# A list scheduler with smaller charges per operation and 90 disturbed restarts

## The chip, the cores and the metric

The kernel runs on all 8 cores of one Trainium2 chip, each on its own 4096 tokens. The metric is the device time of the slowest core, in microseconds (us). The runs of one kernel lie close together: eleven of before took 1242.38 to 1245.46 us. Other runs were slower, most of them with a lower clock on one die: two runs of before, of 1479.74 and 1497.95 us, had 0.81 to 0.84 on cores 4 to 7. Such runs are marked slow and set aside. Cores 0 to 3 are one die and 4 to 7 the other. Each session ran on one chip, with the kernel before beside the others, and only runs of one session are compared.

## The reference

A token mixer (a gated convolution of width 3, and a spatial gating over blocks of 128 positions), an output projection, and a channel mixer with squared ReLU. The argument is about the channel mixer:

```python
h2 = rmsnorm(x, norm2_g[l])                                   # x: (4, 8192, 1024)
a = jax.nn.relu(jnp.einsum('bsd,df->bsf', h2, w_up[l]))       # 1024 -> 4096
x = x + jnp.einsum('bsf,fd->bsd', a * a, w_down[l])           # 4096 -> 1024, plus the residual
...
return rmsnorm(x, final_g)
```

## The kernel before

The program does not write its instruction streams by hand. It declares some thousands of operations with their reads and writes; a list scheduler places them on five queues (TensorE, ScalarE, VectorE, and the POOL and SP queues that issue DMAs). What each operation costs is an estimate in the program:

```python
def act(out, in_, func, reads, writes, n=MT, **kw):
    aps = sum(1 for v in kw.values() if not isinstance(v, (int, float)))
    S.add("act", ..., occ=(n / 1.2 + 200 + 70 * aps) / 1000, ...)     # us; the result is usable 0.09 later

def dve(fn, reads, writes, n=MT, rate=1, src=None):
    S.add("dve", fn, reads=reads, writes=writes, occ=(n / rate + 151) / 960, ...)
```

`occ` is how long the engine is taken and `dur` when the result is usable. A DMA is planned at 290 GB/s, all of them one after another, plus 2 us, plus a margin that the call chooses:

```python
def place(self, ops, phys, lat=0.12, dma_lat=2.0, dma_rate=290e3):    # forward pass
    ...
            if op.dma_key is not None:
                dma_free = max(dma_free, st + op.occ) + op.nbytes / dma_rate
                op.finish = dma_free + dma_lat + op.margin
            else:
                op.finish = st + op.dur - op.occ + occ
```

`place` takes, at each engine's next free moment, the ready operation with the smallest key. `push` runs backward through the order and sets each key to the latest start that still meets the end. The two alternate 9 times and the order with the lowest estimated finish is kept. Of all this only the order goes to the chip: the program writes each engine's list and the semaphores that it waits for.

Two matrix multiplications use a form with 7 products in place of 8, so each weight block of 4 parts must be extended by three VectorE sums to 7. At its first use a block of the down projection comes in as f32 on the POOL queue, is converted to f16 on the way (1 MB of f32 by the program, 512 KB at the destination in the DMA view), summed in place in one of six `RING` buffers and then stored for later:

```python
def combine(p, dst, src, dkeys, reads, margin):
    i, lkey, skey = dkeys
    dma("pool", p[:, 0:4, :, :], src[i % 16]..., reads, p.keys(0, 4), lkey, 4 * 128 * 2048, margin=margin)
    tt(p[:, 4, :, :], p[:, 3, :, :], p[:, 2, :, :], ALU.add, ...)            # "RING <- RING" in the traces
    tt(p[:, 3:6:2, :, :], ..., p[:, 3:5, :, :], ALU.subtract, ...)
    tt(p[:, 6, :, :], p[:, 1, :, :], p[:, 5, :, :], ALU.add, ...)
    dma("sp", dst, p[:, :, :, :], ...)

def load_w(n):
    s, i = wslot(), plan[n]
    if n < 32 and 16 <= i < 24:                       # first use of a down block: load and sum
        combine(RING[s], ws(i), wdn_d, (i, ("fl", s), ("fs", s)), [], 5.0)     # margin 5 us
    else:                                             # stored before: 7 parts, 896 KB, on the SP queue
        dma("sp", RING[s][:, :, :, :], ws(i), ..., margin=2.0)

def load_r(g, o_):                                    # residual: 8 loads a pair of token tiles, into RA and RB
    for h in range(2):
        dma("pool", R[h][:, o_::4, :], x1_d[m]..., ("rl", h, o_), 4 * 128 * 2 * MT, margin=4.0)

def up_unit(q, s):                                    # products into PSUM banks bA, bC, bD
    ...
    prod(bA, P1, True, False); snap(2, bA)            # ScalarE copies the bank to SN
    prod(bD, P2, True, True);  add(2, bD)             # VectorE adds the bank to SN: frees it
    ...
```

The matmuls write into PSUM (PS in the traces), which the program divides into banks; by its semaphores a matmul that is to start a new result waits until its bank has been read out. So VectorE holds two kinds of work in one list: additions that free PSUM banks for TensorE, and weight sums that wait for a DMA.

## Time and profile before

The kernel took 1246.82 us (median of 3, 1246.3 to 1248.05).

| | before |
|---|---|
| TensorE busy, slowest core | 97% of 1244.9 us |
| before the first matmul, all cores | 6.8 to 8.3 us |
| TensorE's stalls and half-clock matmuls before 80 us | 12 to 20 us |
| TensorE's excess from 80 us to the last weight matmul, slowest core | 0.02 us |
| after the last weight matmul | 16.5 to 17.6 us |

The excess is worked out from the trace: the sum, over consecutive matmuls, of the time between their starts less what a matmul needs at a granted clock of 1.00 (in the median 216 ns for 512 columns, 52 ns for 128 and 25 ns for 32, in before). The 5880 matmuls come to some 1200 us. Half-clock matmuls are those at a granted clock of 0.50: on core 7 from 31.70 to 38.53 us, where 512 columns take 427 ns.

From the page of before: busy time, share of the span and instructions of TensorE, then its busy share and its granted clock in tenths over 40 slices.

```profile
PE 1209.6 (97%) x5880; PEld 548.5 (44%) x5880; DVE 893.4 (72%) x1377; ACT 530.4 (43%) x905; POOL 86.0 (7%) x146
...
PE   5899999999999999999999999999999999999994
...
PEclk9899999999999999999999999999999999999998
```

The chain of work that ended last, in order of time (start, us, what), before:

```profile
68.66 1158.35 PE PS L424 x5536
...
1227.10 0.06 DVE RA L439
```

TensorE alone carries the chain from 68.7 to 1227 us.

The table by stage (window, us, busy time and instructions of each engine, granted clock, DMA share, GB/s), core 7:

```profile
core 7: us, PE busy (x) PEld busy (x) DVE busy (x) ACT busy (x) POOL busy (x), PEclk, DMA share, GB/s
...
484.00:491.00 7.00, 7.00 (x34) 3.17 (x33) 5.79 (x9) 3.76 (x7) 0.55 (x1) 1.00 0.99 202
491.00:498.00 7.00, 7.00 (x35) 3.17 (x33) 6.52 (x12) 5.07 (x10) 0.94 (x2) 1.00 0.64 117
```

### The profile page before, as it was taken

To read this page: it belongs to the slowest core of one execution; us is meant where nothing else is said; L and a number is where in the kernel's file an instruction comes from. 1 tells how busy PE (TensorE), PEld (TensorE's weight loads), DVE (VectorE), ACT (ScalarE), POOL (GpSimd) and SP (SyncE) were. 2 spreads that over 40 slices of the span, in tenths; PEclk is the share of its full clock that TensorE was granted. 3 is DMA by queue.
4 is the path that set the end of the run, shared out by engine and by line. 5 is a ranking of instruction groups with operands and counts; after the bars stand their busy time and mean duration, and the time that the engine had idled before them with its cause. 6 is when DMAs were issued, how large, how long until landed. Compare 5 with 4: busy or idle time off the path is not lost.

```text
span 1244.9 us, 18564 instructions; the slowest of 8 cores (1235.7 to 1244.9 us)
## 1 busy us (share of the span) xinstructions
PE 1209.6 (97%) x5880; PEld 548.5 (44%) x5880; DVE 893.4 (72%) x1377; ACT 530.4 (43%) x905; POOL 86.0 (7%) x146
## 2 busy tenths in 40 slices
PE   5899999999999999999999999999999999999994
PEld 3444444444444444444444444444444444444442
DVE  2778687877878887658759737767846876855746
ACT  4544655536554356026127205317405406503524
POOL 0100000000001011000101200000110000110000
PEclk9899999999999999999999999999999999999998
DMA  8968688596675869975577764576984645985423
GB/s 185 171 148 232 167 228 231 148 245 175 179 220 153 279 213 207 237 266 176 169 260 228 262 212 162 211 237 177 295 272 148 216 165 182 279 271 177 149 90 135
DMA packets 55183, 253.81 MB, mean 204 GB/s; under 512 B 6192, under 2 KB 6320, under 8 KB 54832
## 3 DMA queue, kind: packets, MB, share of 16 engines
q1 hardware_dynamic: 35152, 180.27, 42.8%
q0 software_dynamic: 19936, 72.36, 25.3%
q8 instruction: 49, 0.80, 0.3%
q14 instruction: 46, 0.38, 0.1%
HBM read 211.71 MB, written 65.01 MB: 222 GB/s over the span
## 4 chain that ended last, share of the span: by engine, by line
PE 93%; DMA 5%; DVE 1%; issue 0%; SPq 0%; DVEq 0%; POOLq 0%
PE PS L424 93%; DMA WSB_109<-bsf 2%; DMA X_74<-xT 1%; DMA X_73<-xT 1%; DMA WV<-wv 1%; DMA WCXB_53<-wcxb 1%; DVE RA L439 0%; DVE RB L439 0%; SPq L450 0%; DVE WU L446 0%; DVEq L344 0%; DVE FSQ_102 L439 0%; DVE FSQ_101 L439 0%; DVE Z L439 0%; DVEq L284 0%
## 5 line engine op out<-in xcount | busy, mean ns | idle before, releaser
L439 DVE TENSOR_TENSOR RB<-PS,RB 128x512 f32<-128x512 f32 x128 | 87.4, 690 | 91.4 <-PE PS L424 88.9
L424 PE MATMUL PS<-YN,WO 128*128 128x512 f16 x512 | 113.8, 379 | 0.0
L439 DVE TENSOR_TENSOR RA<-PS,RA 128x512 f32<-128x512 f32 x96 | 66.1, 690 | 60.6 <-PE PS L424 59.2
L439 DVE TENSOR_TENSOR A_89<-A_89 128x512 bf16<-128x512 bf16 (+1 forms) x192 | 94.5, 508 | 8.2 <-ACT A_89 L431 3.6
L431 ACT ACTIVATE SN_92<-PS 128x512 f32<-128x512 f32 x63 | 37.4, 595 | 106.5 <-PE PS L424 104.7
L424 PEld LDWEIGHTS PS<-YN,WO 128*128 128x128 f16 x512 | 50.1, 98 | 60.4
L424 PE MATMUL PS<-A_89,RING_83 128*128 128x512 bf16 x308 | 76.1, 379 | 0.0
L424 PE MATMUL PS<-A_89,RING_85 128*128 128x512 bf16 x308 | 76.1, 379 | 0.0
L424 PE MATMUL PS<-A_89,RING_86 128*128 128x512 bf16 x308 | 75.8, 379 | 0.0
L424 PE MATMUL PS<-A_89,RING_84 128*128 128x512 bf16 x308 | 75.5, 379 | 0.0
L424 PE MATMUL PS<-H_96,RING_87 128*128 128x512 f16 x308 | 75.1, 379 | 0.0
L424 PE MATMUL PS<-H_96,RING_83 128*128 128x512 f16 x308 | 74.5, 379 | 0.0
L424 PE MATMUL PS<-H_96,RING_88 128*128 128x512 f16 x308 | 74.3, 379 | 0.0
L424 PE MATMUL PS<-H_96,RING_84 128*128 128x512 f16 x308 | 74.3, 379 | 0.0
L431 ACT ACTIVATE SN_90<-PS 128x512 f32<-128x512 f32 x66 | 39.2, 595 | 76.7 <-PE PS L424 75.6
L424 PE MATMUL PS<-A_89,RING_88 128*128 128x512 bf16 x280 | 69.4, 379 | 0.0
L424 PE MATMUL PS<-A_89,RING_87 128*128 128x512 bf16 x280 | 69.1, 379 | 0.0
L431 ACT ACTIVATE SN_93<-PS 128x512 f32<-128x512 f32 x64 | 38.2, 596 | 71.8 <-PE PS L424 71.3
L424 PE MATMUL PS<-H_96,RING_85 128*128 128x512 f16 x280 | 67.9, 379 | 0.0
L424 PE MATMUL PS<-H_96,RING_86 128*128 128x512 f16 x280 | 67.4, 379 | 0.0
L431 ACT ACTIVATE SN_91<-PS 128x512 f32<-128x512 f32 x63 | 37.5, 595 | 70.1 <-PE PS L424 68.0
L439 DVE TENSOR_TENSOR SN_92<-PS,SN_92 128x512 f32<-128x512 f32 x63 | 43.4, 690 | 27.4 <-PE PS L424 22.7
(231 smaller groups left out, 2029.2 us busy)
## 6 DMA issues: line engine op xcount, KB each, us to landing
RING_83<-ws_s SPq DMA_DIRECT2D x21, 896.0 KB, 6.0
RING_84<-ws_s SPq DMA_DIRECT2D x21, 896.0 KB, 6.4
RING_87<-ws_s SPq DMA_DIRECT2D x20, 896.0 KB, 5.3
RING_88<-ws_s SPq DMA_DIRECT2D x20, 896.0 KB, 6.2
RING_85<-ws_s SPq DMA_DIRECT2D x19, 896.0 KB, 6.0
RING_86<-ws_s SPq DMA_DIRECT2D x19, 896.0 KB, 6.3
ws_s<-PREP_65 SPq DMA_DIRECT2D x12, 896.0 KB, 6.3
ws_s<-PREP_66 SPq DMA_DIRECT2D x12, 896.0 KB, 5.6
```

The costliest lines, as they stand in the source:

```text
L424: ins = e.matmul(real(o_), lhsT=l, rhs=r, start=st, stop=sp, skip_group_check=True)
L431: S.add("act", lambda e: e.activation(out=out, in_=real(in_), func=func, **kw), reads=reads, writes=writes, occ=(n / 1.2 + 200 + 70 * aps) ...
L439: dve(lambda e: e.tensor_tensor(out=out, in0=real(in0), in1=in1, op=op), reads, writes, n, rate, in0)
```

## The change

The intent is a truer model and a better search. The charge of a VectorE operation on 512 f32 elements goes from 691 to 601 ns, and of a ScalarE operation from 627 to 497 ns. The time until a result is usable is kept (780 and 717 ns). Then the best order's keys are disturbed 90 times with a spread of 0.3 us, and the lowest estimated finish wins. No instruction, byte or buffer is added or removed; only orders, PSUM banks and waits move.

```diff
-    def schedule(self, phys, rounds=8):
+    def schedule(self, phys, rounds=8, tries=90):
...
+        rnd = random.Random(1)
         best = None
-        for _ in range(rounds + 1):
...
+        for t in range(tries + 1):
+            if t:
+                for o, k in best[5].items():
+                    o.key = k if o.fixed else k + rnd.gauss(0, 0.3)
+            for _ in range(3 if t else rounds + 1):
...
+                order = self.place([op for op, _ in base], phys)
+                if len(order) < len(base):
+                    break
+                est = max(o.finish for o in order)
+                if best is None or est < best[0]:
+                    best = (est, order, ..., keys)
+                self.push(order, est)
...
-        assert len(order) == len(ops)
...
-                  occ=(n / 1.2 + 200 + 70 * aps) / 1000, banks=...)
+                  occ=(n / 1.2 + 70 + 70 * aps) / 1000, dur=(n / 1.2 + 290 + 70 * aps) / 1000,
+                  banks=...)
...
-            S.add("dve", fn, reads=reads, writes=writes, occ=(n / rate + 151) / 960,
-                  banks=...)
+            S.add("dve", fn, reads=reads, writes=writes, occ=(n / rate + 65) / 960,
+                  dur=(n / rate + 237) / 960, banks=...)
```

More of the change, by code (lines that the diff above doesn't have):

```diff
@@ L1 @@
 import contextlib
+import random
 import numpy as np
@@ L110, in add @@
         return op
-    def schedule(self, phys, rounds=8):
+    def schedule(self, phys, rounds=8, tries=90):
         base = [(op, op.deps) for op in self.ops]
+        rnd = random.Random(1)
         best = None
-        for _ in range(rounds + 1):
-            for op, deps in base:
-                op.deps = deps
-                for b in op.banks:
-                    b.left = len(b.ops)
-            order = self.place([op for op, _ in base], phys)
-            est = max(o.finish for o in order)
-            if best is None or est < best[0]:
-                best = (est, order, [(o, o.deps) for o in order],
-                        [(o.opens, o.opens.phys) for o in order if o.opens is not None],
-                        {o: (o.start, o.finish) for o in order})
-            self.push(order, est)
+        for t in range(tries + 1):
[3 more added lines that the diff above has]
+            for _ in range(3 if t else rounds + 1):
+                for op, deps in base:
+                    op.deps = deps
+                    for b in op.banks:
+                        b.left = len(b.ops)
+                keys = {op: op.key for op, _ in base}
+                order = self.place([op for op, _ in base], phys)
[3 more added lines that the diff above has]
+                if best is None or est < best[0]:
+                    best = (est, order, [(o, o.deps) for o in order],
+                            [(o.opens, o.opens.phys) for o in order if o.opens is not None],
+                            {o: (o.start, o.finish) for o in order}, keys)
+                self.push(order, est)
         self.est_total, self.ops = best[:2]
@@ L431, in act @@
             S.add("act", lambda e: e.activation(out=out, in_=real(in_), func=func, **kw), reads=reads, writes=writes,
-                  occ=(n / 1.2 + 200 + 70 * aps) / 1000, banks=[in_.bank] if isinstance(in_, Late) else [])
+                  occ=(n / 1.2 + 70 + 70 * aps) / 1000, dur=(n / 1.2 + 290 + 70 * aps) / 1000,
+                  banks=[in_.bank] if isinstance(in_, Late) else [])
         def dve(fn, reads, writes, n=MT, rate=1, src=None):
-            S.add("dve", fn, reads=reads, writes=writes, occ=(n / rate + 151) / 960,
-                  banks=[src.bank] if isinstance(src, Late) else [])
+            S.add("dve", fn, reads=reads, writes=writes, occ=(n / rate + 65) / 960,
+                  dur=(n / rate + 237) / 960, banks=[src.bank] if isinstance(src, Late) else [])
         def tt(out, in0, in1, op, reads, writes, n=MT, rate=1):
```

## The prediction

> **What bounds the kernel now.** TensorE, almost perfectly. The page's busy line gives it 97% of 1244.9 us, but matmul records overlap (379 ns each), so I read start-to-start times in the trace of the slowest core. From 80 us to the last weight matmul at 1227.5 us, a 512-column matmul follows its predecessor after about 216 ns; the total excess there is 0.02 us. At that pace the 5880 matmuls add up to 1200 us. The other 45 us are edges: 7.9 us before the first matmul, 20 us of stalls and half-clock matmuls before 80 us, 17.4 us of tail after the last weight matmul. On other cores the startup excess is 12 to 18 us, the tail 16.5 to 17.6. VectorE (72%) and ScalarE (43%) have slack: in the stage table VectorE is busy 301 of 378 us at its fullest.
>
> **What the change does.** It adds and removes no instruction, byte or buffer. It changes numbers of the program's own scheduler, hence the order on each engine, the PSUM banks and the waits. VectorE's charge for a 512-element f32 operation falls from 691 to 601 ns, ScalarE's from 627 to 497; the time until a result is usable stays (780 and 717 ns). Then the best order is disturbed 90 times and the lowest modelled finish kept.
>
> **Is the new charge truer?** Yes. VectorE's 512-element f32 operations reading PSUM have records of 691 ns but, when dense, 598 to 601 ns start-to-start; ScalarE's 597 and 478 ns (PSUM), 627 and 519 ns (SBUF). [...] One charge becomes too small: a 384-element weight scaling is charged 168 ns and takes 228.
>
> **How much lies on the critical path.** In the middle 1150 us, nothing: the chain of waits shows one run of matmuls from 68.7 to 1227 us, and no order changes their pace. Only edges can gain.
> - Startup: DMA engines are 93 to 100% busy from 8 to 72 us and weight loads are issued in a fixed chain, so the longest stalls (3.1 us for a convolution weight, 2.2 us for the u weight) end with a landing plus a scaling. Order can remove perhaps 1 to 3 us, such as a u scaling stuck behind a bias addition that waited for a late load. But the scheduler assumes 290 GB/s where startup moves 156 to 203, so its gains carry over poorly: -1.5 us.
> - Tail: final stores fill the DMA engines from 1230.6 to 1241.5 us. The first half stored starts being scaled at 1228.6, though its sums were ready by 1225; an earlier start is worth at most 2.5 us: -1 us.
> - Middle: less slack could open short stalls: +0.2 us.
>
> The optimum is a model's, and the slowest of eight cores decides.
>
> **Predicted time.** 1244.0 us against 1246.82; 8 in 10 within 1238.0 to 1249.0. Faster by over 2%: 2%; within 2%: 96%; slower by over 2%: 2%.
>
> **What would show it.** Right: instruction counts and mean durations unchanged; TensorE's excess between 80 us and the last weight matmul under 1 us; startup excess and tail each shorter by 0 to 3 us. Wrong: matmul gaps waiting for VectorE or ScalarE in the middle (model too optimistic), or startup excess moving by over 5 us (order matters there more than DMA).
>
> **What would make it wrong.** An order with waits for late loads ahead of needed VectorE work, holding TensorE or dropping its clock, or PSUM banks reused too tightly: 5 to 20 us lost. A gain over 2% would need 25 of the 45 edge microseconds.

The dropping clock can be seen in the trace of before: on core 7 the granted clock was 0.50 from 31.70 to 38.53 us, during and after a stall of TensorE of 2.90 us (by the view) that ended at 33.63.

## More of the kernel before

Below, a load lands when the last of its data is reported to be in place (its landing is given in us after its issue), and the slack behind it is the time from there to the first instruction that needs it.

What POOL issued before that, in the timeline of before (start, us, queue, line, operation, tiles, count, idle time before and what ended it):

```profile
463.50 2.84 POOL L450 DMA_DIRECT2D RB<-x_s  x4 [29.67 <-PE PS L424]
466.33 1.41 POOL L450 DMA_DIRECT2D RA<-x_s  x2
468.80 0.70 POOL L450 DMA_DIRECT2D RA<-x_s  x1 [1.06 <-DMA x_s<-X_74]
473.44 0.57 POOL L450 DMA_DIRECT2D RING_86<-wdn  x1 [3.93 <-PE PS L424]
474.01 0.70 POOL L450 DMA_DIRECT2D RA<-x_s  x1
```

SP's timeline in the same stretch, before:

```profile
452.67 0.32 SPq L450 DMA_DIRECT2D RING_84<-ws_s  x1
```

The DMA issues of 445 to 475 us, before (tiles, queue, operation, count, KB each at the destination, us from issue to landing):

```profile
RING_84<-ws_s SPq DMA_DIRECT2D x1, 896.0 KB, 5.7
RING_86<-wdn POOLq DMA_DIRECT2D x1, 512.0 KB, 14.8
```

VectorE's timeline when it comes to the first sum of this block, before:

```profile
492.98 0.69 DVE L439 TENSOR_TENSOR SN_90<-PS,SN_90 128x512 f32<-128x512 f32 x1
493.58 0.42 DVE L439 TENSOR_TENSOR RING_86<-RING_86 128x512 f16<-128x512 f16 x1
```

Seven residual loads go out ahead of the first down weights. The weights land at 473.44 + 14.8 = 488.2 us; VectorE comes to their first sum at 493.58, 5.3 us later, and no idle time stands beside it. That gap does not show as a cost or as a gain in any summary. It is slack.

The other cores of this profile have less of it. On core 0 the first down weights took 24.2 us and the second block's 24.4, and TensorE stalled there for 2.78 us, at a granted clock that stayed at 1.00, waiting for the second block itself:

```profile
494.98 1.89 PE L424 MATMUL PS<-A_89,RING_85 128*128 128x512 bf16 x8 [2.61 <-DMA RING_85<-wdn]
```

(The view counts the gap from the modelled end of the last matmul; the stalls in the text are start to start, less 216 ns, and so 0.16 to 0.17 us longer.)

## The result, and the profile after

The kernel after took 1251.88 us in the median of its three fast runs (1251.07, 1251.88 and 1253.61; with one slow run of 1338.3 the median is 1252.74, and a fifth run, 1283.38, was slow too). Before took 1247.13 beside it (1246.3 to 1248.05, 4 runs). The ratio is 1.004, with a 95% interval of 1.0021 to 1.006. Ratios are the mean time of one kernel's fast runs over that of the other's of the same rounds, so not quite the ratio of the medians. The kernel became about 5 us slower, and the predicted gain of 2.8 us and range up to 1249 did not hold.

The page of after, the slowest core (core 2, 1249.5 us). 67 matmul records are missing, so its busy time is not compared with before's.

```profile
PE 1205.5 (96%) x5813; PEld 548.4 (44%) x5880; DVE 896.7 (72%) x1377; ACT 527.3 (42%) x905; POOL 85.5 (7%) x146
...
PE   5899999999999998999999999999999999999994
...
PEclk9899999999999999999999999999999999999997
```

One slice of TensorE's row, the sixteenth (468 to 500 us), dropped from 9 to 8. In the waits of after (engine and tile that waited, for what: us in total, times, longest us), two lines are new:

```profile
DVE RING_86 L449 <- DMA RING_86<-wdn: 5.9, 1, 5.9
...
PE PS L433 <- DVE SN_90 L449: 5.7, 1, 5.7
```

The chain of after in that stretch, in order of time (lines of the program are 9 or 10 further down than before):

```profile
439.80 26.35 PE PS L433 x122
...
466.70 28.07 DMA RING_86<-wdn
...
494.94 0.06 DVE RING_86 L449
...
496.57 0.61 DVE SN_90 L449
...
497.31 3.57 PE PS L433 x8
```

The chain leaves TensorE, goes through one weight load of 28.1 us, then four VectorE operations (the first and the last of them are shown), and only then returns. VectorE's timeline of after shows the order:

```profile
488.32 0.69 DVE L449 TENSOR_TENSOR SN_90<-PS,SN_90 128x512 f32<-128x512 f32 x1 [1.41 <-ACT SN_91 L440]
494.94 0.43 DVE L449 TENSOR_TENSOR RING_86<-RING_86 128x512 f16<-128x512 f16 x1 [5.92 <-DMA RING_86<-wdn]
...
496.48 0.68 DVE L449 TENSOR_TENSOR SN_90<-PS,SN_90 128x512 f32<-128x512 f32 x1
```

The first sum of the weights stands ahead of additions that free PSUM banks. The load is late, VectorE idles 5.92 us in front of work that was ready, and TensorE runs out of banks. TensorE's timeline of after:

```profile
489.71 1.89 PE L433 MATMUL PS<-H_96,RING_84 128*128 128x512 f16 x8
497.31 1.87 PE L433 MATMUL PS<-H_96,RING_83 128*128 128x512 f16 x4 [5.71 <-DVE SN_90 L449]
```

VectorE did not go around the sum in these 5.92 us, though the inputs of the additions behind it, at 495.28 and 496.48 in its timeline, were there: TensorE's last matmul ended at 491.60, and ScalarE had written SN_91 by 488.26.

The table by stage, after, core 2:

```profile
core 2: us, PE busy (x) PEld busy (x) DVE busy (x) ACT busy (x) POOL busy (x), PEclk, DMA share, GB/s
484.00:491.00 7.00, 7.00 (x34) 3.14 (x32) 3.61 (x8) 3.90 (x8) 0.53 (x1) 1.00 0.99 160
491.00:498.00 7.00, 1.29 (x5) 0.38 (x4) 3.06 (x6) 1.94 (x4) 0.00 (x0) 0.86 0.58 115
498.00:505.00 7.00, 6.78 (x22) 2.62 (x22) 4.45 (x9) 1.41 (x3) 0.53 (x1) 0.65 0.85 219
```

In the 7 us after the stall TensorE is busy but starts 22 matmuls where before it started 34: the granted clock is 0.65. In the trace it is 0.50 from 496.01 to 502.84 us and 1.00 on both sides, and while it is 0.50 the 512-column matmuls start 427 ns apart in place of 216. Other cores of this profile: a stall of 4.07 us (core 3) came with 6.83 us at 0.50, one of 4.57 us (core 5) with 3.41 us, and those of 2.44 us (core 4), 1.11 (core 7) and 1.04 (core 1) with none. Over the profiles of all runs, after 80 us: all 29 stalls of 3.41 us or more dropped the clock to half, for 3.4, 6.8 or 10.2 us; of the seven from 2.69 to 3.37 us two did (2.77 and 3.27) and five did not (2.69, 2.78, 2.80, 3.18 and 3.37). In startup the clock fell after a shorter one too: on core 7 of before it was 0.50 from 69.25 to 72.66 us, after a stall that the view gives as 2.03 us and that ended at 68.66. So the stall of 5.88 us cost more than itself: some ten matmul starts 427 ns apart are 2 us more. On this core the excess of the middle is 8.75 us, with another stall, of 1.13 us at 923 us, in it.

What was issued before it. POOL's timeline of after, core 2:

```profile
457.19 2.84 POOL L460 DMA_DIRECT2D RB<-x_s  x4 [31.06 <-PE PS L433]
460.02 1.41 POOL L460 DMA_DIRECT2D RA<-x_s  x2
461.92 1.41 POOL L460 DMA_DIRECT2D RA<-x_s  x2 [0.48 <-DVE SN_90 L449]
466.70 0.55 POOL L460 DMA_DIRECT2D RING_86<-wdn  x1 [3.38 <-PE PS L433]
```

SP's timeline of after:

```profile
463.62 0.32 SPq L460 DMA_DIRECT2D RING_84<-ws_s  x1
```

The DMA issues of 445 to 475 us, after:

```profile
RING_84<-ws_s SPq DMA_DIRECT2D x1, 896.0 KB, 14.4
RING_86<-wdn POOLq DMA_DIRECT2D x1, 512.0 KB, 28.1
```

The new order issues all eight residual loads before the first down weights, where the old one had seven, and the 896 KB load of the SP queue now falls into this burst instead of 11 us before it. The weights take 28.1 us where they took 14.8 (on core 2 of before 16.8). In this first profile six of eight cores stall here by over 1 us: core 2 by 5.88, core 5 by 4.57, core 3 by 4.07, core 4 by 2.44, core 7 by 1.11, core 1 by 1.04; cores 0 and 6 not at all, and these have the shortest spans, 1235.3 and 1238.2 us.

### The profile page after: what moved, and what is told of

Same layout as the page of the kernel before. It is cut to its first block, busy times and chain, and to the rows that moved or that the text cites. A ratio compares the mean times of both kernels' runs of the same rounds, so it can differ in the third digit from the quotient of the medians.

```text
span 1249.5 us, 18484 instructions; the slowest of 8 cores (1235.3 to 1249.5 us)
## 1 busy us (share of the span) xinstructions
PE 1205.5 (96%) x5813; PEld 548.4 (44%) x5880; DVE 896.7 (72%) x1377; ACT 527.3 (42%) x905; POOL 85.5 (7%) x146
## 3 DMA queue, kind: packets, MB, share of 16 engines
q0 software_dynamic: 19936, 72.36, 26.3%
## 4 chain that ended last, share of the span: by engine, by line
PE 92%; DMA 6%; DVE 1%; issue 1%; DVEq 0%; ACT 0%; SPq 0%; POOLq 0%; ACTq 0%
PE PS L433 92%; DMA RING_86<-wdn 2%; DMA RING_83<-ws_s 1%; DMA X_73<-xT 1%; DMA WCXB_52<-wcxb 1%; DMA X_74<-xT 1%; DMA WCXB_51<-wcxb 0%; DVE RA L449 0%; DVE RB L449 0%; ACT RS_79 L440 0%; DVE SN_90 L449 0%; DVE HT_64 L449 0%; DVEq L353 0%; DVE RING_86 L449 0%; SPq L460 0%
```

## The experiments

Four sessions, on four chips. The theory: the late first down weights, in front of bank-freeing additions, hold TensorE. The rivals: the longer wait is a sign of general tightness and many small losses; the edges (startup, and the final stores) lost the time; or the search, and not the charges, brought it.

Before the runs, the plan itself. The program's scheduler prints what it expects; these are the plan's numbers and not times of the chip. For the first down weights:

| plan of | estimated finish | landing after issue, with the 5 us margin | first sum after issue | slack |
|---|---|---|---|---|
| before | 1224.85 | 16.0 | 20.8 | 4.8 |
| after | 1223.46 | 21.7 | 22.4 | 0.7 |
| smaller charges alone | 1224.98 | 21.7 | 21.8 | 0.1 |
| disturbed restarts alone | 1224.03 | 17.4 | 21.1 | 3.7 |

The whole change bought 1.4 us in the plan and let the slack behind this load go from 4.8 to 0.7 us. The plan sees a landing that is later by 5.6 us, and takes that as good enough.

Most edited kernels below use one helper, put in after the scheduling, which moves operations within the finished order and keeps every dependency and wait:

```diff
         S.schedule(PS)
+        def move(group, anchor, after=True):
+            rest = [o for o in S.ops if o not in group]
+            i = rest.index(anchor) + after
+            S.ops = rest[:i] + group + rest[i:]
+            at = {o: n for n, o in enumerate(S.ops)}
+            assert all(at[d] < at[o] for o in S.ops for d in o.deps)
+            S.by_eng = {e: [o for o in S.ops if o.eng == e] for e in ENGS}
+        fl = [o for o in S.ops if o.dma_key and o.dma_key[0] == "fl"]     # first loads of down weights
+        by_idx = {o.idx: o for o in S.ops}
```

### First session: the parts of the change, and the queue

Before took 1244.53 us here (11 runs, 1242.38 to 1245.46).

**after_again**: the kernel after, unchanged.

> The changed kernel once more, as the reference for the others on this chip. Theory L (late landing): the loss comes from one place near 490 us. Two down-projection weight loads queue behind eight residual loads, land 20 to 28 us after their issue on most cores, and VectorE, in program order, waits for them ahead of additions that free the PSUM banks TensorE needs. L expects 0.3 to 0.6% over before and, on most cores, a TensorE stall of 1 to 6 us near 490 us. Rival E (edges: startup or tail lost by the new order) expects the loss with no such stall on the slowest core.

The fast runs were 1255.07, 1247.89 and 1247.75, the other three slow: ratio 1.0047 (1.0025 to 1.007). In its profile all eight cores stall at the same place, by 1.8 to 4.8 us. The loss repeats on another chip.

**charges_only**: the smaller charges without the restarts.

```diff
-    def schedule(self, phys, rounds=8, tries=90):
+    def schedule(self, phys, rounds=8, tries=0):
```

> Only the lower charges, no disturbed tries. In the scheduler's plan the first sum follows the planned landing (5 us margin included) by 0.2 us, against 4.8 us in before and 0.7 us in the changed kernel. Theory L expects the same stall of 1 to 6 us near 490 us and 0.3 to 0.6% over before. Rival R (the random search overfits the model, the charges are harmless) expects before's time within 0.1%.

Ratio 1.0037 (1.002 to 1.0054), fast runs 1246.72 to 1253.22. Cores 0, 1, 5 and 7 stall at 488 to 491 us by 2.42, 4.36, 4.44 and 3.43 us, the others not at all. Core 5 of this run, the timeline of VectorE:

```profile
493.40 0.42 DVE L449 TENSOR_TENSOR RING<-RING 128x512 f16<-128x512 f16 x1 [6.59 <-DMA RING<-wdn]
```

Its ScalarE and its TensorE, from their timelines:

```profile
494.52 0.63 ACT L440 ACTIVATE SN<-SN 128x512 f32<-128x512 f32 x1 [6.35 <-DVE SN L449]
```

```profile
495.77 4.44 PE L433 MATMUL PS<-H,RING 128*128 128x512 f16 x12 [4.27 <-ACT SN L440]
```

The plan's slack is 0.12 us here; the expectation gives it as 0.2. TensorE names ScalarE as what it waited for, ScalarE names VectorE, and VectorE the load. A table of waits alone would blame ScalarE; the chain has to be followed to its root. The charges alone bring the stall.

**tries_only**: the restarts with the old charges.

```diff
-                  occ=(n / 1.2 + 70 + 70 * aps) / 1000, dur=(n / 1.2 + 290 + 70 * aps) / 1000,
+                  occ=(n / 1.2 + 200 + 70 * aps) / 1000,
...
-            S.add("dve", fn, reads=reads, writes=writes, occ=(n / rate + 65) / 960,
-                  dur=(n / rate + 237) / 960, banks=...)
+            S.add("dve", fn, reads=reads, writes=writes, occ=(n / rate + 151) / 960, banks=...)
```

> Only the 90 disturbed tries, old charges. The planned gap between landing and first sum is 3.7 us. Theory L expects little stall near 490 us, at most 1 to 2 us on one or two cores, and a time within 0.2% of before. Rival R expects the whole loss, 0.3 to 0.6%.

The four runs in the fast state were 1243.61, 1244.48, 1246.55 and 1249.46; their mean, 1246.0, is 0.14% over before's 1244.3. The ratio given for the run, 1.0052 (1.0009 to 1.0095), does not follow from these four, and 1262.62, a run marked slow, seems to be in it; I don't rest anything on it. Stalls at this place were 2.33, 0.65 and 1.43 us on cores 5, 6 and 7 and none on the other five; on cores 5 and 7 TensorE waited for the second block of weights itself, and on no core did VectorE wait for the first. So the restarts alone do not bring the wait that the charges alone bring, as the slack in the plans has it (3.7 against 0.1 us). That they also cost less time (0.14 against 0.37%) is not shown: the fast runs overlap, 1243.61 to 1249.46 against 1246.72 to 1253.22.

**after_ra_later**: the kernel after with four of the eight residual loads, the ones that are needed last, moved behind the first two loads of down weights. Everything else, VectorE's order too, stays.

```diff
+        late = [o for o in S.ops if o.dma_key and o.dma_key[0] == "rl" and o.dma_key[2] >= 2 and o.start < fl[1].start]
...
+        move(late, fl[1])
```

> The changed kernel's order with one edit: four of the eight residual loads, needed some 25 us later, are issued after the first two down-projection weight loads instead of before them. All other instructions keep their order. Theory L expects those weight loads to land 8 to 15 us sooner, no stall over 0.5 us between 485 and 500 us on any core, and 4 to 6 us off the changed kernel: 1245 to 1248 us. Rival E expects the changed kernel's time within 1 us.

The first down weights landed 7.5 to 15.3 us after their issue on the eight cores, and no core stalled near 490 us. The same places of the timelines, core 1, POOL:

```profile
455.88 1.43 POOL L460 DMA_DIRECT2D RB<-x_s  x2 [31.05 <-PE PS L433]
458.88 1.41 POOL L460 DMA_DIRECT2D RA<-x_s  x2 [1.56 <-DVE SN L449]
465.39 0.55 POOL L460 DMA_DIRECT2D RING<-wdn  x1 [5.11 <-PE PS L433]
```

and VectorE:

```profile
487.62 0.42 DVE L449 TENSOR_TENSOR RING<-RING 128x512 f16<-128x512 f16 x1
```

With four loads ahead instead of eight, the sum starts without idle time, in the same position of the list. That takes the wait away by its cause. The time went from 1.0047 to 1.002 (1.0003 to 1.0036) of before, so about 0.27%; in the session of this run alone that is not clear of the noise (fast runs of 1244.05 to 1251.0 against 1247.75 to 1255.07), and the fourth session repeats it. It did not go wholly to before: core 5, the slowest in the profile, had stray stalls of 1.41 and 2.27 us at 1085 and 1107 us, and tails were 17.3 to 20.5 us.

### Second session: does the position of the sums matter?

Before was scattered on this chip (fast runs 1244.95 to 1251.07, and two of eleven slow), so small ratios say little; the traces say more.

**before_again**: before unchanged, one look.

> The kernel before, unchanged, for a profile on this chip to set the others against. Both theories expect the first profile's picture: no TensorE stall over 0.4 us between 80 us and the last weight matmul on most cores, last output store issued 10.7 to 10.9 us after the last weight matmul.

1249.47 us. Cores 0, 4, 5 and 6 stall by 0.74, 0.54, 1.29 and 1.54 us near 495 us, TensorE waiting for the weights themselves. The wait is for the second block, as on core 0 of before's first profile: in before's order such a stall is that block's landing less 21.4 to 21.6 us. So before is not free of late landings, but its VectorE never held TensorE there.

**after_sums_later**: in the order of after, the sums of the first two blocks are moved later in VectorE's list, behind the additions.

```diff
+        sums = [[by_idx[fl[n].idx + j] for j in (1, 2, 3, 4)] for n in (0, 1)]
+        move(sums[1], next(o for o in S.ops if o.eng == "dve" and o.start > 484.2))
+        move(sums[0], next(o for o in S.ops if o.eng == "dve" and o.start > 486.3))
```

> The changed kernel's order, but the sums that VectorE forms from the first two down-projection weight loads are put several operations later in VectorE's order; the loads keep their place. If only VectorE's place in line mattered, the stall near 490 us goes to zero. Theory L (the loads land late, and TensorE itself needs the second of them about 4 us after the first sum) expects the stall to shrink but not to vanish: on cores where the changed kernel would lose 4 to 6 us, 2 to 4 us remain, and now TensorE waits for the load itself. Time 1 to 3 us under the changed kernel.

Ratio 1.0013 (0.9977 to 1.0049), unclear. VectorE no longer holds TensorE in front of the first sum, but on four cores TensorE now comes to the second block of weights before it is there: stalls of 0.41 to 3.27 us, the longest where the first load took 27.1 us and the second 25.7. The edit also made a stall of its own, 1.0 to 1.4 us at 497 to 506 us on every core, where TensorE waits for VectorE. On the core with the longest landing the two come to 4.3 us, where a landing of 27.1 us costs 4.9 in the order of after (see the next run). So with this landing the position of the sums alone recovers little, as expected. This run is inconclusive on the time.

**before_sum_early**: the mirror image. In the order of before the first sum alone is moved about 6 us earlier in the plan; on the chip VectorE comes to it 14.9 us after the issue instead of 20.15.

```diff
+        move([by_idx[fl[0].idx + 1]], next(o for o in S.ops if o.eng == "dve" and o.start > 473.0))
```

> The converse on the kernel before: the first of those sums is put about 6 us earlier in VectorE's order, nothing else. The wait is now reached some 14 us after the load's issue, where before's loads took 13 to 24 us to land. Theory L expects TensorE stalls of 1 to 6 us near 485 us on most cores where there were none, and 1 to 5 us over before. Rival E expects no change.

Ratio 1.0008 (0.9983 to 1.0033): the 1 to 5 us over before that were expected are not shown, and before itself stalls on four cores of this chip. What the run shows is in the trace. Stalls of 3.41, 1.72, 1.69 and 2.02 us on cores 0, 2, 5 and 7; none on four cores, where the load had landed within 14.5 us. VectorE of core 0 in this run:

```profile
483.71 0.68 DVE L439 TENSOR_TENSOR SN<-PS,SN 128x512 f32<-128x512 f32 x1
489.04 0.43 DVE L439 TENSOR_TENSOR RING<-RING 128x512 f16<-128x512 f16 x1 [4.65 <-DMA RING<-wdn]
```

On each of the four TensorE waited for VectorE, by way of ScalarE, and VectorE for the load, which no core of before's two profiles shows. So the wait can be put into before by taking its slack, on half of the cores rather than on most as expected. On those cores the stall is the landing less 16.1 us, within 0.1 us (19.5, 17.8, 17.8 and 18.1 us gave 3.41, 1.72, 1.69 and 2.02). In the order of after it is the landing less 22.2 us: landings of 20.6, 23.2, 24.6, 26.3, 26.8 and 28.1 us gave stalls of 0, 1.04, 2.44, 4.07, 4.57 and 5.88. So each of these two orders has a time at which it needs the load, and in these landings every microsecond beyond it was a microsecond of TensorE.

**after_fixed**: the moved residual loads, and one halving of VectorE in the tail moved ahead of the scaling before it, since the last store of after is issued 11.96 us after the last weight matmul, where before it was 10.73 to 10.89.

```diff
...
+        move(late, fl[1])
+        dve_ = S.by_eng["dve"]
+        h = max(n for n, o in enumerate(dve_) if abs(o.occ - (256 + 65) / 960) < 1e-6)
+        move([dve_[h]], dve_[h - 1], after=False)
```

> The changed kernel with two edits of order: the four residual loads after the first two down-projection weight loads, as in the run that did this alone, and in the tail VectorE's last halving of squares one scaling earlier, since in the changed order three scalings stand ahead of it where before has two. Expected: no stall over 0.5 us near 490 us, last store issued about 10.8 us after the last weight matmul instead of 11.96, and the time within 0.15% of before. If the rest of the loss lies elsewhere, it stays 2 us over before.

Ratio 0.9975 (0.9955 to 0.9994), the last store at 10.66 to 10.83 us. No core stalled at 490 us, but cores 4 and 5 did at 503 to 508 us, by 0.7 to 1.9 us, where the next loads are needed. It looked like a version that beats before; the fourth session tried it again.

### Third session: harder edits

Before took 1245.37 us (1243.85 to 1247.99).

**after_third**: the kernel after.

> The changed kernel a third time, as the reference of these four runs on one chip. Theory L: TensorE stalls of 1 to 6 us near 490 us on most cores, 0.2 to 0.6% over before.

Ratio 1.0018 (1.0005 to 1.0031). Stalls of 4.18, 4.35 and 3.53 us on cores 1, 5 and 7, 0.8 and 1.12 on two others, none on three. The smallest loss that unchanged after showed goes with a profile in which only three cores stall by over 1.2 us.

**after_fixed2**: the four residual loads moved behind the first four weight loads, with the tail's edit; **before_fixed**: the same move of the loads in the order of before.

```diff
+        move(late, fl[3])
```

> The changed kernel's order with the four residual loads moved behind the first FOUR down-projection weight loads (the run that moved them behind the first two left two cores with stalls of 0.7 to 2.5 us on the fourth), and the halving in the tail one scaling earlier. Theory L expects no TensorE stall over 0.5 us between 480 and 515 us on any core and a time 3 to 6 us under the changed kernel on the same chip, level with before or up to 0.3% under it.

> The same move of the four residual loads in the kernel before; its tail is left alone. It shows what the change itself is worth once the late landing is out of both orders. Theory L expects no stall near 490 us and 0 to 0.2% under before; if the truer charges and the search gain anything on the chip, the repaired changed kernel is at least 1 us under this one, else the two are level.

Both are misses. after_fixed2 gave 1.0049 (1.0025 to 1.0074) and before_fixed 1.0057 (1.0041 to 1.0074). The first four loads now land early (5 to 16 us in after_fixed2), and the next one behind the moved residual loads is late. VectorE of core 6 in after_fixed2:

```profile
503.62 0.69 DVE L449 TENSOR_TENSOR RA<-PS,RA 128x512 f32<-128x512 f32 x1 [0.24 <-PE PS L433]
516.13 0.42 DVE L449 TENSOR_TENSOR RING<-RING 128x512 f16<-128x512 f16 x1 [11.82 <-DMA RING<-wdn]
```

TensorE stalls by 1.6 to 9.7 us, from 504 to 509 us on, on seven of eight cores of after_fixed2, and by 4.48, 5.16, 5.82 and 4.65 us, from 508 to 512 us on, on four cores of before_fixed. The bytes of the burst did not go away when they were put back; they met the next consumer (11.82 us of VectorE above). As a measure the miss is useful: four cores of before_fixed that stall by about 5 us, in before's own order and with its own edges, cost 0.57%.

**after_margin12**: the change whole, with the margin of these weight loads raised from 5 to 12 us and everything scheduled anew.

```diff
-                combine(RING[s], ws(i), wdn_d, (i, ("fl", s), ("fs", s)), [], 5.0)
+                combine(RING[s], ws(i), wdn_d, (i, ("fl", s), ("fs", s)), [], 12.0)
```

> The repair in the scheduler itself: charges and tries as in the change, but the allowance added to these weight loads' landing raised from 5 to 12 us, so that the plan has the first sum 26 us after the load's issue instead of 22.4. Everything is reordered. Theory L expects stalls of at most 2 us near 490 us on the cores whose load takes over 26 us, and a time within 0.2% of before.

1244.98 us (1243.51 to 1249.42), ratio 1.0001 (0.9987 to 1.0015). The loads took up to 25.2 us, but the plan now has the sums of the first three blocks 26.1 to 27.6 us after the issue, and VectorE waits for no load. A wait of 0.82 us of TensorE for a sum was left on every core. The plan's finish is 1224.97, so the 1.4 us that the change had bought are given back, and the chip's loss of 0.18% in these rounds with them.

### Fourth session: what was still open

By then one chip had shown a version faster than before, and the tail's part was unknown. Before took 1246.81 us (1242.61 to 1248.94).

**after_fourth**: the kernel after; **after_tail**: the tail's edit alone; **after_ra_later_b** and **after_fixed_b**: the two kernels of before, repeated.

```diff
+        move([dve_[h]], dve_[h - 1], after=False)      # after_tail: this alone
```

> The changed kernel, as the reference of these four runs on one chip: TensorE stalls near 490 us on most cores and 0.2 to 0.6% over before.

> The changed kernel's order with the tail edit alone (VectorE's last halving of squares one scaling earlier). The last store should be issued 10.7 us after the last weight matmul instead of 11.96; the stall near 490 us stays. If the tail's order costs what the issue times say, 0.5 to 1.3 us under the changed kernel; if the stores' drain hides it, level with it.

> The move of four residual loads behind the first two weight loads, once more. Theory L expects the stall near 490 us gone from the cores that have it in the changed kernel and 2 to 5 us off it; what stays over before is the tail and stray stalls of 1 to 3 us.

> Both edits once more, to see whether 0.9975 against before holds on another chip. If it does, the ratio is under 0.999; if that was the chip's disturbed state, 0.999 to 1.002. Against the changed kernel both readings expect 3 to 5 us less.

| | ratio to before | 95% interval | stalls near 490 us |
|---|---|---|---|
| after_fourth | 1.0041 | 1.0022 to 1.006 | 4.28, 5.36, 2.69, 1.97, 5.31, 2.00 on six cores |
| after_tail | 1.0026 | 1.0004 to 1.0048 | 1.5 to 6.0 stay on six cores; stray ones of 6.27 and 5.57 at 1088 and 1091 us on the two slowest cores |
| after_ra_later_b | 1.0003 | 0.9984 to 1.0022 | none at 490; 0.6 to 1.9 on two cores at 497 to 507 us |
| after_fixed_b | 1.0021 | 1.0001 to 1.0042 | not the same: stray ones, of 5.61 at 722 us on the slowest core and 3.18 at 1090 us on core 0 |

Moving four DMA issues takes 0.38% of the 0.41% away, and the fast runs do not overlap: 1244.14 to 1248.79 against 1249.98 to 1252.21. The tail's edit issued the last store at 10.7 us as wanted, and changed the time by -0.15% on its own and by +0.18% on top of the other, both within the noise: nothing is shown for it. The 0.9975 of after_fixed did not hold on another chip. No version here clearly beats before.

### The profiles pooled

Fast profiles of the first down weights, all cores. They are of different chips, and before's tail alone went from 17.1 us in its first profile to 18.8 in its second, so the last three rows show little by themselves:

| | before (2 profiles) | after (4) | after_ra_later (2) |
|---|---|---|---|
| residual loads ahead of it in the POOL queue | 7 | 8 | 4 |
| landing after its issue, mean (range), us | 16.7 (12.7 to 24.2) | 24.3 (16.5 to 28.1) | 12.5 (7.5 to 15.3) |
| first residual issue to this landing, us | 26.6 | 33.8 | 22.1 |
| moved by the DMA engines in that time, GB/s | 222 | 224 | 232 |
| cores that stall over 0.4 us near 490 us | 5 of 16 | 25 of 32 | 2 of 16 |
| cores with a granted clock below 0.97 there | 0 | 13 of 32 | 0 |
| TensorE's excess in the middle, mean, us | 0.72 | 2.98 | 0.14 |
| TensorE's stalls before 80 us, mean, us | 15.6 | 15.1 | 14.9 |
| tail after the last weight matmul, mean, us | 17.9 | 17.7 | 18.8 |
| span, mean of cores, us | 1241.6 | 1243.1 | 1241.1 |

The rate is nearly the same in all three, so a later landing means more bytes ahead of it. From before to after the stretch grew by 7.2 us, which at 223 GB/s is 1.6 MB; one more residual load (0.5 MB) and the 0.9 MB load of the SP queue make 1.4 MB. The traces count it by queue: from the first residual issue to the landing after moves 0.9 MB more on SP's queue than before and 0.8 MB more on POOL's. What the SP load alone costs was not tried. On core 2 of after the SP load was issued behind all eight residual loads, at 463.62 us, and landed at 478.0 us, ahead of the last four of them (481.4 to 492.3); its own landing went from 5.7 us after its issue (before, core 7) to 14.4 when it fell into the burst. POOL's residual and down weight loads landed among themselves in the order of their issue on all 16 cores of the first profiles of before and after, on this core 1.3 to 5.5 us apart.

From before to after the mean span grew by 1.5 us: the middle gave +2.26, the stalls before 80 us -0.5, the tail -0.2. The two first profiles alone say the same (+2.3 us: +2.5, -0.1 and -0.3). The stalls cost more than the middle's sum shows: on cores without any, after's middle is 0.76 us shorter than before's, mostly because its order goes over from 512- to 128-column matmuls 24 times where before does so 27 times. (In the traces of both a 128-column matmul starts 309 ns after a 512-column one, where another of 512 starts after 216; on the way back it is 152 ns instead of 52. So a change there and back costs about 0.19 us.) The time of the kernel is that of the slowest core, and grew by some 5 us, since the stalls fall unevenly: in three of after's four profiles the slowest core is the one with the longest stall near 490 us.

## Why the prediction was wrong

- **TensorE bounds the kernel: right.** The middle of before is matmul after matmul at 216 ns, and nothing in the runs made that pace faster, but for the 0.76 us just named.
- **The new charges are truer: right, and of no use.** Dense VectorE additions out of PSUM start 598 to 601 ns apart and the new charge is 601. (The 144 scalar_tensor_tensor operations of the same size are charged 601 too and start 658 ns apart, so for them it is too small.) But the charge was wrong in a place that did not bound anything, and its excess had worked as slack.
- **Startup, -1.5 us, and tail, -1 us: small.** The means over cores moved by -0.5 and -0.2 us, less than they differ between chips. The last store is even issued 1.1 us later after the last weight matmul than before. Since the mean tail did not grow and taking that away changed nothing clear, I can't say that it costs.
- **The failed step: "Middle: less slack could open short stalls: +0.2 us."** This term was mis-sized by a factor of over ten. It measured +2.26 us in the mean of all cores, 8.75 us on the slowest core of the first profile (0.02 before), and about 5 us in the kernel's time. The sentence before it, "In the middle 1150 us, nothing", and "Only edges can gain" are right about gains and were read as though they held for losses. Under what would make it wrong, the prediction named "An order with waits for late loads ahead of needed VectorE work, holding TensorE or dropping its clock": that is what happened, and it was given far too small a chance.
- **What was missed to size it.** The trace of before had the numbers. The load landed at 488.2 us and its sum came at 493.58 on the slowest core, so 5.3 us of slack stood in front of VectorE; on other cores landings reached 24.2 us. The program plans DMAs at 290 GB/s and the burst runs at 222. And the prediction itself used that difference, but for startup only. In before the sum is planned 20.8 us after the issue and the load took 16.7 on average: 4.1 us to spare. In after it is planned at 22.4 and took 24.3: 1.9 us short.
- **The rivals.** The general tightness fell: moving four DMA issues, with VectorE's order untouched, took the stall away on all cores in two sessions (in the second two cores stall by less than 2 us a little later), and in one of them the time clearly with it. The search as the only culprit fell: the charges alone bring the same wait and 1.0037; the restarts alone do not bring the wait. The edges are not shown to lose anything.

The stray stalls have the same look at other places. At 1080 to 1100 us VectorE of after waits for a residual load in front of an addition that frees a bank; after_tail, core 6, VectorE and then TensorE:

```profile
1088.95 0.69 DVE L449 TENSOR_TENSOR RA<-PS,RA 128x512 f32<-128x512 f32 x1 [6.54 <-DMA RA<-x_s]
```

```profile
1094.23 4.12 PE L433 MATMUL PS<-A,RING 128*128 128x512 bf16 x12 [6.11 <-DVE RB L449]
```

Over 0.4 us this happens on 15 of the 88 cores in the profiles of after's order and its edits, and on none of 32 in before's. The one at 722 us is such a wait too. At 414 us VectorE waits for a store, in front of what TensorE needs; at 915 and 1107 us TensorE waits for stored weights itself, as before's order also does at 629 and 824 us. No edit tried any of these places.

Left open: why those loads are late in single profiles; why one core of a pair stalls and its neighbour often does not; the SP load's own part; and the slow state, which met 9 of 25 runs of after and 2 of 49 of before in these sessions. Nothing here explains that count and no conclusion rests on it.

## What to carry to other kernels

When a schedule is made from a model, what it leaves idle is not all waste: an estimate that is too high for one resource can be the only reserve behind another that is estimated too low. Before trading it, list every wait of an engine on a DMA, compare the measured landings of all cores (not their mean) with the moment the engine gets there, and put the reserve where it belongs, into the load's own margin: 12 us instead of 5 brought this change back to level (1.0001 of before). Here an operation that waited for a late load held up the ready work behind it that frees the bottleneck's buffers (in after VectorE idled 5.92 us and TensorE 5.71); and issuing the burst in another order helped only until the next consumer (in after_fixed2 VectorE idled 11.82 us there).
